# A hybrid attention block on one core: the gate and up products of the FFN on scaled fp16 halves instead of fp32r halves

## The chip, the cores and the metric

The kernel runs on one core of a Trainium2 chip, as one program. The metric is the time of one execution on the device in microseconds (us). Three runs of the kernel before gave 3368.54, 3373.79 and 3376.36 us; the median is 3373.79. The profile is of one execution more, of 3371.81 us.

## What is computed

One layer of an encoder over 2048 tokens and 16 meta tokens that are put ahead of them, 1024 wide, all in float32. The reference, cut to its structure:

```python
h = rms_norm(x, attn_norm_g)
proj = h @ w_in                        # 1024 -> 2304
out_a = grouped-query attention        # 8 query heads, 2 key/value heads, 64 wide
out_b = differential attention         # 4 heads of two 64-wide halves, values 128 wide
x = x + concat(out_a, out_b) @ w_out   # 1024 -> 1024
h = rms_norm(x, ffn_norm_g)
g = h @ w_gate                         # 1024 -> 2816
u = h @ w_up                           # 1024 -> 2816
x = x + (silu(g) * u) @ w_down         # 2816 -> 1024
return x without the meta tokens
```

## The kernel before

The kernel has four stages, one after the other: the input projection with norms and rotary embedding, the attention, the output projection (lines 1204 to 1261) and the FFN (lines 1262 to 1350). The change touches the last two.

**Products in halves.** A float32 product is made of three products of halves: each operand is kept as a rounded copy ("high") and the rest ("low", the operand minus the copy), and high x high, low x high and high x low are summed in PSUM; low x low is left out. In the attention the halves are fp16, with values scaled into its range. In the projections and the FFN they are fp32r, the four-byte type that TensorE takes in one pass. `split` (line 114) forms them: a cast on one engine (line 112 is the copy) and a subtraction on another (line 116). `transpose_split` (line 124) does so behind a transpose on TensorE (line 129).

**Output projection.** It goes through 16 tiles of 128 tokens (`for t in range(NT)`, line 1231). `load_t` (line 369) has SP load the mixed attention rows (mix_scr) and x of a tile, 512 KB each, into two pairs of buffers. `prep` (line 1215), for tile t+1 while tile t is multiplied, scales the rows on ACT (line 1216), squares half of them (line 1218), normalises that half on VectorE and POOL (lines 1220 to 1224), and transposes and splits the rows. A tile's products are 48 matmuls of 128x512 (line 1240) in two halves of 512 columns; VectorE adds x (line 1251). The first 8 tiles of y stay in SBUF, are normalised by `norm` (line 1198, with the FFN's gain g2, loaded once on line 1213) and turned into `h2h` and `h2l` (lines 1181 and 1182), the transposed halves that are the moving operand of the FFN. The last 8 tiles go to HBM (y_scr, line 1261) for the second half of the FFN.

**FFN.** Two passes (b) of 1024 tokens, each through 22 blocks (f) of 128 columns of w_gate and w_up. For a block `wload` (line 1278) has SP load three weight tiles of 512 KB (gate, up, down) and forms their halves, with the cast on ACT and the subtraction on POOL. For each half of 512 tokens (n) gate and up are 24 matmuls each of 128x512 (line 1332): 8 slices of the 1024-wide input, three terms each. The weights are the stationary operand, h2h and h2l the moving one. Tanh on ACT (line 1334) and two operations on VectorE (lines 1335 and 1336) make silu(g) * u, which is split again. The products with w_down (line 1293) of block f-1 follow, in groups of three, each ended by an addition to y on VectorE (line 1295). In numbers: 2 x 22 x 2 x 2 x 24 = 4224 matmuls on line 1332 and 2112 on line 1293.

```python
for ps, w in ((pg, wg), (pu, wu)):
    for k in range(KD):
        for ii, (a, b_) in enumerate(((w[0], hh[n]), (w[0], hl[n]), (w[1], hh[n]))):
            T.matmul(ps, a[:, k], b_[:, k], start=(k == 0 and ii == 0), stop=(k == KD - 1 and ii == 2))
th = tp4.tile([P, 512], F32, name="th4")
A.activation(th, pg, AF.Tanh, scale=0.5)
```

**What sets the order.** The attention's order is written by a planner in the file, which ends before the output projection. From there on each engine's order is fixed when the program is built, from the order of the text and a model of what is ready when; work may be put far ahead of its place in the text where a buffer is free (the loads of y_scr on line 1308 stand in block 17 of the text and are issued in block 0). On the chip each engine goes through its order strictly. SP issues all loads and stores of these stages in one order. Buffers of the weights go round in rings (line 1264): four for halves of gate and up (two blocks), four for raw loads, which begin with the buffers of the last two tiles of the output projection.

Of the kernel before, what the change touches and what calls it, by code (L numbers as in the profile page):

```python
# [11 lines left out]
F32 = mybir.dt.float32  # L12
F32R = mybir.dt.float32r
F16 = mybir.dt.float16
BF16 = mybir.dt.bfloat16
I32 = mybir.dt.int32
AF = mybir.ActivationFunctionType
ALU = mybir.AluOpType
AX = mybir.AxisListType
PSUM = bass.MemoryType.PSUM  # L20

P = 128
D = 1024
# [3 lines left out]
NT = S // P  # L27
NC = NT + 1
HD = 64
KD = D // P  # L30
UW = 384
DFF = 2816
# [53 lines left out]
def block_kernel(ctx: ExitStack, tc: tile.TileContext, x, meta, g1, w_in, gpack, lam4, subln,  # L86
# [27 lines left out]
    def split(hi, lo, src, hi_eng, lo_eng):  # L114
        copy(hi_eng, hi, src)
        lo_eng.tensor_tensor(out=lo, in0=src, in1=hi if hi.dtype == F16 else hi.bitcast(F32), op=ALU.subtract)  # L116
# [261 lines left out]
    with ExitStack() as ph:  # L378
# [774 lines left out]
        while True:  # L1153
# [11 lines left out]
            t, n, z = best  # L1165
# [10 lines left out]
    with ExitStack() as ph:  # L1176
# [1 line left out]
        TB = NT // 2  # L1178
        HT = TB // 2
        y = {t: yp.tile([P, D], F32, name=f"y{t}") for t in range(TB)}  # L1180
        hh = [yp.tile([P, KD, HT * P], F32R, name=f"h2h{i}") for i in range(2)]
        hl = [yp.tile([P, KD, HT * P], F32R, name=f"h2l{i}") for i in range(2)]
        g2_sb = yp.tile([P, D], F32, name="g2_sb")

        def normed(np_, yt, h):
# [19 lines left out]
        with ExitStack() as p3:  # L1205
# [6 lines left out]

            SP.dma_start(g2_sb, g2.partition_broadcast(P))

            def prep(t, mx):
                A.activation(mx[:, :512], mx[:, :512], AF.Copy, scale=ivs)
                sq = sqp.tile([P, 512], F32, name="sq")
                A.activation(sq, mx[:, 512:], AF.Square)
                ss = sm.tile([P, 4], F32, name="ss3")
                V.tensor_reduce(ss, sq.rearrange("p (h d) -> p h d", d=P), axis=AX.X, op=ALU.add)  # L1220
                rs = inv_rms(sm, ss, ivn, P, 4, "b")
                bv = mx[:, 512:].rearrange("p (h d) -> p h d", d=P)
                V.tensor_tensor(out=bv, in0=bv, in1=rs.unsqueeze(2).broadcast_to([P, 4, P]), op=ALU.mult)
                V.scalar_tensor_tensor(bv, bv, ivs, gb.unsqueeze(1).broadcast_to([P, 4, P]), op0=ALU.mult, op1=ALU.mult)
                mh, ml = halves(ering[t % 2])
                transpose_split(psT, mx, P, mh, ml)
                return mh, ml
# [2 lines left out]
            pend = []  # L1230
            for t in range(NT):
                mh, ml, xt = cur
                if t + 1 < NT:
                    if t + 1 not in mxt:
                        load_t(t + 1, SP)
                    nxt = mxt[t + 1]
# [25 lines left out]
        with ExitStack() as p4:  # L1262
# [4 lines left out]
            def place(ring, shape, dtype):  # L1267
                tag = rings[ring].pop(0)
                rings[ring].append(tag)
                return slot(tag, shape, dtype)  # L1270
# [6 lines left out]

            def wload(src, name):
                dn = name == "d"
                w = place("d" if dn else "w", [P, 2, 1, D] if dn else [P, 2, KD, P], F32R)  # L1280
                raw = place("r", [P, 1, D] if dn else [P, KD, P], F32)
                SP.dma_start(raw[:, 0] if dn else raw, src)
                split(w[:, 0], w[:, 1], raw, A, G)
                return w[:, 0], w[:, 1]

# [26 lines left out]
            for b in range(2):  # L1312
                for f in range(NF):
# [8 lines left out]
                    for n in range(2):  # L1322
# [8 lines left out]
                                for ii, (a, b_) in enumerate(((w[0], hh[n]), (w[0], hl[n]), (w[1], hh[n]))):  # L1331
                                    T.matmul(ps, a[:, k], b_[:, k], start=(k == 0 and ii == 0), stop=(k == KD - 1 and ii == 2))  # L1332
                        th = tp4.tile([P, 512], F32, name="th4")
                        A.activation(th, pg, AF.Tanh, scale=0.5)  # L1334
                        V.scalar_tensor_tensor(th, th, 1.0, pg, op0=ALU.add, op1=ALU.mult)
                        V.scalar_tensor_tensor(th, th, 0.5, pu, op0=ALU.mult, op1=ALU.mult)
                        split(ah[:, ns], al[:, ns], th, A, G)
                        if b == 0 and f == NF - 1:
                            for t in range(TB + n * HT, TB + (n + 1) * HT):
# [82 lines left out]
```

## Time and profile before

| what | us |
|---|---|
| median of 3 runs | 3373.79 |
| lowest and highest run | 3368.54, 3376.36 |
| profiled execution | 3371.81 |
| its span in the profile | 3369.9 |
| TensorE busy in it | 3211.7 |
| VectorE, ACT, POOL busy | 2051.8, 1488.2, 1660.6 |

The profile counts an engine as busy while an instruction of it is under way. Matmuls are pipelined: one record lasts from its start to its own end, some 395 ns for 128x512 in fp32r, while the next begins much earlier. What a matmul takes of the engine is therefore read as the distance of two starts in an unbroken run, or as the length of such a run by its count. The granted clock of TensorE is given as a share of the upper of its two levels, 2.4 GHz. A wait is put down to what came last by the profile.

### The profile page before, as it was taken

What the parts mean: (1) busy time and instruction counts of PE and PEld (TensorE: products, weight loads), DVE (VectorE), ACT (ScalarE), POOL (GpSimd) and SP (SyncE); (2) the same over time, 40 slices, a digit from 0 to 9 for tenths busy, and PEclk for the clock granted to TensorE, in tenths of its full rate; (3) what the DMA queues carried; (4) which work ended last, traced back from release to release, by engine and by line L of the source; (5) the groups of instructions that cost most, each with busy time, mean ns of one, the idle gap of its engine ahead of it and who ended that gap; (6) DMA issues with size and microseconds to landing.
All of it is one profiled execution on the core that took longest, in us unless ns stands there. A gap on an engine that the chain in (4) does not pass through costs nothing.

```text
span 3369.9 us, 57645 instructions
## 1 busy us (share of the span) xinstructions
PE 3211.7 (95%) x23041; PEld 2483.7 (74%) x23041; DVE 2051.8 (61%) x3640; ACT 1488.2 (44%) x1839; POOL 1660.6 (49%) x1596
## 2 busy tenths in 40 slices
PE   9999988989988998888799999999999999999999
PEld 7999975555555555555588888888887888888887
DVE  7555578888889888888764244444445434444445
ACT  6333338988887788788732211111112211111110
POOL 6887867776676777767510323232323232323231
PEclk9999989999999999999899999999999999999999
DMA  5222232443443334333533411111112411111111
GB/s 174 69 69 67 61 87 69 87 108 77 94 114 75 72 92 103 75 85 77 124 116 119 132 38 57 38 57 38 57 38 69 155 46 44 50 44 51 43 44 50
DMA packets 498749, 258.27 MB, mean 77 GB/s; under 512 B 330192, under 2 KB 478112, under 8 KB 497968
## 3 DMA queue, kind: packets, MB, share of 16 engines
q1 hardware_dynamic: 496768, 252.07, 28.3%
q8 instruction: 181, 2.97, 0.4%
q10 hardware_dynamic: 1712, 2.51, 0.3%
q14 instruction: 88, 0.72, 0.1%
HBM read 145.38 MB, written 39.93 MB: 55 GB/s over the span
## 4 chain that ended last, share of the span: by engine, by line
PE 77%; DVE 11%; ACT 6%; issue 4%; DMA 2%; POOL 1%; SPq 0%; DVEq 0%; ACTq 0%; POOLq 0%
PE pg L1332 29%; PE psd L1293 14%; PE pl L269 11%; PE ps L1240 5%; PE sy L482 4%; PE ob L594 3%; PE oa L570 3%; DVE e L489 3%; ACT et L555 2%; DVE mna L502 2%; PE sy L498 2%; PE sy L512 2%; DVE e L536 2%; PE sy L513 2%; PE pt L129 1%
## 5 line engine op out<-in xcount | busy, mean ns | idle before, releaser
L1295 DVE TENSOR_TENSOR y<-psd,y 128x512 f32<-128x512 f32 x704 | 484.9, 691 | 607.5 <-PE psd L1293 604.8
L1332 PE MATMUL pg<-h2h,e 128*128 128x512 f32 x2112 | 692.4, 395 | 0.0
L561 POOL TENSOR_TENSOR hl<-et,hl 128x1024 f16<-128x1024 f32 (+1 forms) x247 | 520.2, 2125 | 307.8 <-ACT hl L112 177.7
L1332 PEld LDWEIGHTS pg<-h2h,e 128*128 128x128 f32 x2112 | 396.8, 188 | 96.0
L1332 PE MATMUL pg<-h2l,e 128*128 128x512 f32 x1056 | 417.4, 395 | 0.0
L1334 ACT ACTIVATE th<-pg 128x512 f32<-128x512 f32 x88 | 52.6, 598 | 816.5 <-PE pg L1332 814.5
L116 POOL TENSOR_TENSOR e<-qa,e 128x1024 fp32r<-128x1024 f32 x44 | 106.4, 2417 | 516.2 <-issue 426.3
L489 DVE CUSTOM_DVE_ANT_0 e<-sy,zero,mn 128x1024 f32<-128x1024 f32 x256 | 325.7, 1277 | 42.7 <-PE sy L482 37.6
L555 ACT ACTIVATE et<-sy,lnpa,ndq 128x1024 f32<-128x1024 f32 (+1 forms) x288 | 321.9, 1144 | 42.2 <-PE sy L513 22.3
L549 POOL TENSOR_TENSOR p<-e,p 128x516 f16<-128x516 f32 (+2 forms) x320 | 311.1, 1004 | 50.1 <-ACT p L112 48.9
L502 DVE TENSOR_REDUCE mna<-sy 128x1 f32<-128x1024 f32 x256 | 311.5, 1218 | 16.4 <-PE sy L498 15.8
L482 PE MATMUL sy<-kt,qb 128*128 128x512 f16 (+1 forms) x1280 | 284.2, 342 | 30.2 <-DVE mn L489 9.9
L570 PEld LDWEIGHTS <-hl 128*128 128x128 f16 (+1 forms) x6528 | 241.9, 98 | 95.9 <-issue 23.9
L517 ACT ACTIVATE e<-e,bs,ndq 128x2064 f32<-128x2064 f32 x128 | 269.2, 2103 | 92.3 <-DVE bs L522 92.1
L116 POOL TENSOR_TENSOR kt<-qb,kt 128x1024 fp32r<-128x1024 f32 x22 | 53.1, 2414 | 490.4 <-issue 430.1
L570 PE MATMUL oa<-va,hl 128*128 128x65 f16 (+3 forms) x6528 | 261.9, 194 | 24.7 <-DVE hl L561 9.3
L1293 PE MATMUL psd<-e,e 128*128 128x512 f32 x1056 | 282.5, 395 | 0.7 <-DVE y L1295 0.7
L1293 PE MATMUL psd<-kt,kt 128*128 128x512 f32 x1056 | 282.6, 395 | 0.0
L112 ACT CAST hl<-et 128x1024 f16<-128x1024 f32 (+1 forms) x288 | 275.8, 991 | 7.9 <-PE oa L570 6.4
L594 PEld LDWEIGHTS <-pt 128*128 128x128 f16 (+2 forms) x3200 | 201.8, 98 | 71.4 <-issue 7.4
L1332 PEld LDWEIGHTS pg<-h2l,e 128*128 128x128 f32 x1056 | 198.4, 188 | 48.2
L594 PE MATMUL ob<-vb,pt 128*128 128x128 f16 (+2 forms) x3200 | 232.9, 220 | 0.0
(208 smaller groups left out, 5917.2 us busy)
## 6 DMA issues: line engine op xcount, KB each, us to landing
qa<-in_w_gate_dram SPq DMA_DIRECT2D x22, 512.0 KB, 3.9
qa<-in_w_down_dram SPq DMA_DIRECT2D x22, 512.0 KB, 3.6
qb<-in_w_up_dram SPq DMA_DIRECT2D x22, 512.0 KB, 3.8
qa<-in_w_up_dram SPq DMA_DIRECT2D x22, 512.0 KB, 3.8
qb<-in_w_down_dram SPq DMA_DIRECT2D x22, 512.0 KB, 3.6
qb<-in_w_gate_dram SPq DMA_DIRECT2D x22, 512.0 KB, 3.8
raw<-in_w_in_dram SPq DMA_DIRECT2D x48, 192.0 KB, 3.4
xt<-in_x_dram SPq DMA_DIRECT2D x16, 512.0 KB, 3.8
```

What stands on the lines that cost most here:

```text
L269: T.matmul(ps[:rows, c0:UW], hb[:, a, k, :rows], w_at(w, ui, k)[:, c0:], start=(k == 0 and a == 0 and w == 0), stop=(k == KD - 1 and a == 1))
L482: T.matmul(y[:, (c - c0) // 512 if g_ else j, :n], qt[:, j, a, qi * P:(qi + 1) * P], kt[:, c:c + n], start=(a == 0), stop=(a == 1))
L489: V.tensor_tensor_reduce(e[:, c0:c1], src[:, :c1 - c0], zero.broadcast_to([P, c1 - c0]), 1.0, mn[:, g_ - 1:g_] if g_ else big, ALU.add, AL ...
L502: V.tensor_reduce(g["mn"][:, h, g_:g_ + 1], y.rearrange("p b n -> p (b n)"), axis=AX.X, op=ALU.min)
L549: eng.tensor_tensor(out=p[:, at + c0:at + c1], in0=st["e"][0][:, c0:c1], in1=p[:, c0:c1], op=ALU.subtract)
L555: A.activation(of(et, k), of(y, k), AF.Exp, bias=lnpa if k else lnpa[:NM], scale=ndq[:, 0:1] if k else ndq[:NM, 0:1])
L561: eng.tensor_tensor(out=of(z[:, 1], k), in0=of(et, k), in1=of(z[:, 0], k), op=ALU.subtract)
L570: T.matmul(o[:, h, :wn], z[:rows, a, i, h * P:(h + 1) * P], vt[:rows, c, vh, :wn], start=(first and h == 0 and n == 0), stop=(last and n = ...
L594: T.matmul(o, pt[:rows, blk, :], vt[:rows, c, vh, :], start=(c == 0 and n == 0), stop=(c == NC - 1 and n == 1))
L1293: T.matmul(ps, a[:, i * P:(i + 1) * P], w[:, 0, ns], start=(ii == 0), stop=(ii == 2))
L1295: V.tensor_tensor(out=yt[:, ns], in0=ps, in1=yt[:, ns], op=ALU.add)
L1332: T.matmul(ps, a[:, k], b_[:, k], start=(k == 0 and ii == 0), stop=(k == KD - 1 and ii == 2))
```

## The change

The halves of h2 become fp16 instead of fp32r, and so do the halves of the gate and up weights; the down products stay as they are. To fit fp16's range the gain g2 is scaled to 2^9 by its largest magnitude, rounded to a power of two (eight VectorE operations behind the load of g2, five of them on one column), and the weights are multiplied by a power of two, made from the sum of squares of both matrices. That sum is formed during the output projection: `squares` loads half a 128-row slice of w_gate and of w_up (128x1408 each) into one of two buffers and squares it on ACT with an accumulated sum; it is called for four slices in the first two tiles and for one in each of the next twelve, 16 calls with 32 loads. `weights_scale`, in the last but one tile, sums over partitions by a matmul with ones and forms the scale and its inverse. Each gate and up load then has one more pass on ACT that scales it in place. Tanh and the product behind it take the inverse scale as an operand instead of a constant.

```diff
-        hh = [yp.tile([P, KD, HT * P], F32R, name=f"h2h{i}") for i in range(2)]
-        hl = [yp.tile([P, KD, HT * P], F32R, name=f"h2l{i}") for i in range(2)]
+        hh = [yp.tile([P, KD, HT * P], F16, name=f"h2h{i}") for i in range(2)]
+        hl = [yp.tile([P, KD, HT * P], F16, name=f"h2l{i}") for i in range(2)]
...
+            V.tensor_reduce(gm2[:, 0:1], g2_sb, axis=AX.X, op=ALU.max)
+            V.tensor_reduce(gm2[:, 1:2], g2_sb, axis=AX.X, op=ALU.min)
...
+            V.tensor_scalar(g2_sb, g2_sb, gm2[:, 1:2], 2.0 ** 9, op0=ALU.mult, op1=ALU.mult)
+            wqp = p3.enter_context(tc.tile_pool(name="wqp", bufs=2, reuse_waits="tile"))
+            psS = p3.enter_context(tc.tile_pool(name="psS", bufs=1, space=PSUM, reuse_waits="tile"))
+
+            def squares(t):
+
+                rs_, cs_ = slice(t // 2 * P, (t // 2 + 1) * P), slice(t % 2 * (DFF // 2), (t % 2 + 1) * (DFF // 2))
+                for i, w in enumerate((w_gate, w_up)):
+                    raw = wqp.tile([P, DFF // 2], F32, name="wq")
+                    SP.dma_start(raw, w[rs_, cs_])
+                    A.activation(raw, raw, AF.Square, accum_out=wsq[:, t, i:i + 1])
+
+            def weights_scale():
+
+                tot = np3.tile([P, 1], F32, name="tot")
+                V.tensor_reduce(tot, wsq.rearrange("p t i -> p (t i)"), axis=AX.X, op=ALU.add)
+                ps = psS.tile([P, 1], F32, name="pss")
+                T.matmul(ps, allones, tot, start=True, stop=True)
+                V.tensor_scalar(tot, ps, 1e-30, None, op0=ALU.max)
+                G.tensor_tensor(out=wsc[:, 0:1], in0=tot, in1=mhalf[:, :1], op=ALU.pow)
...
+                V.reciprocal(wsc[:, 1:2], wsc[:, 0:1])
+                V.tensor_scalar(unh[:, 0:1], wsc[:, 1:2], gm2[:, 0:1], 2.0 ** -10, op0=ALU.mult, op1=ALU.mult)
+                V.tensor_scalar(unh[:, 1:2], unh[:, 0:1], unh[:, 0:1], 2.0, op0=ALU.mult, op1=ALU.mult)
...
             for t in range(NT):
                 mh, ml, xt = cur
+                for z in (2 * t, 2 * t + 1) if t < 2 else (t + 2,):
+                    if z < NT:
+                        squares(z)
+                if t == NT - 2:
+                    weights_scale()
...
-                w = place("d" if dn else "w", [P, 2, 1, D] if dn else [P, 2, KD, P], F32R)
+                w = place("d" if dn else "w", [P, 2, 1, D] if dn else [P, 2, KD, P], F32R if dn else F16)
                 raw = place("r", [P, 1, D] if dn else [P, KD, P], F32)
                 SP.dma_start(raw[:, 0] if dn else raw, src)
+                if not dn:
+                    A.activation(raw, raw, AF.Copy, scale=wsc[:, 0:1])
                 split(w[:, 0], w[:, 1], raw, A, G)
...
-                        A.activation(th, pg, AF.Tanh, scale=0.5)
+                        A.activation(th, pg, AF.Tanh, scale=unh[:, 0:1])
                         V.scalar_tensor_tensor(th, th, 1.0, pg, op0=ALU.add, op1=ALU.mult)
-                        V.scalar_tensor_tensor(th, th, 0.5, pu, op0=ALU.mult, op1=ALU.mult)
+                        V.scalar_tensor_tensor(th, th, unh[:, 1:2], pu, op0=ALU.mult, op1=ALU.mult)
```

## Rows read from the trace of the kernel before

**Rows 1.** The page, part 1: engine, busy us, share of the span, instructions.
```profile
PE 3211.7 (95%) x23041; PEld 2483.7 (74%) x23041; DVE 2051.8 (61%) x3640; ACT 1488.2 (44%) x1839; POOL 1660.6 (49%) x1596
```
**Rows 2.** The page, part 4: the chain that ended last, shares by line.
```profile
PE pg L1332 29%; PE psd L1293 14%; PE pl L269 11%; PE ps L1240 5%; PE sy L482 4%; PE ob L594 3%; PE oa L570 3%; DVE e L489 3%; ACT et L555 2%; DVE mna L502 2%; PE sy L498 2%; PE sy L512 2%; DVE e L536 2%; PE sy L513 2%; PE pt L129 1%
```
**Rows 3.** Stretches: length, then PE, PEld, DVE, ACT, POOL busy, clock, DMA share, GB/s.
```profile
1688.70:1878.10 189.40, 189.16 (x913) 155.80 (x913) 95.34 (x153) 54.88 (x93) 26.73 (x25) 1.00 0.35 116
1878.10:3369.90 1491.80, 1485.27 (x6403) 1196.56 (x6401) 624.01 (x913) 251.22 (x337) 426.70 (x227) 1.00 0.19 57
```
**Rows 4.** Groups of line 1332 by form: busy us, mean ns of one, idle before.
```profile
L1332 PE MATMUL pg<-h2h,e 128*128 128x512 f32 x2112 | 692.4, 395 | 0.0
...
L1332 PE MATMUL pg<-h2l,e 128*128 128x512 f32 x1056 | 417.4, 395 | 0.0
...
L1332 PE MATMUL pg<-h2h,kt 128*128 128x512 f32 x704 | 228.1, 395 | 0.0
...
L1332 PE MATMUL pg<-h2l,kt 128*128 128x512 f32 x352 | 139.3, 396 | 0.0
```
**Rows 5.** The chain in order of time, in the FFN: start us, us, what.
```profile
1878.75 44.82 PE pg L1332 x192
```
**Rows 6.** Timeline of TensorE in the attention: start us, us, instruction; eight starts lie between.
```profile
527.85 0.38 PE L512 MATMUL sy<-qa,kt 128*128 128x512 f16 x1 [0.29 <-ACT et L555]
...
529.57 0.62 PE L570 MATMUL oa<-va,hl 128*128 128x65 f16 x15
```
**Rows 7.** A stretch of the attention around them, columns as in rows 3.
```profile
500.00:540.00 40.00, 32.80 (x336) 18.31 (x335) 34.38 (x59) 36.29 (x35) 26.10 (x19) 0.96 0.19 45
```
**Rows 8.** The chain in order of time, in the input projection.
```profile
120.41 4.20 PE pl L269 x24
```
**Rows 9.** Groups of ACT by form: the Squares and Exp that accumulate.
```profile
L517 ACT ACTIVATE e<-e,bs,ndq 128x2064 f32<-128x2064 f32 x128 | 269.2, 2103 | 92.3 <-DVE bs L522 92.1
...
L1200 ACT ACTIVATE h_f<-y 128x1024 f32<-128x1024 f32 x8 | 8.6, 1070 | 0.0
...
L1200 ACT ACTIVATION_READ_ACCUMULATOR h_f<-y 128x1 f32 x8 | 1.6, 197 | 0.0
```
**Rows 10.** Timeline of all engines in the output projection, one tile's preparation.
```profile
1813.48 1.04 PE L129 MATMUL pt<-ident,qa 128*128 128x128 f32 x8
...
1814.58 0.32 SPq L376 DMA_DIRECT2D qa<-mix_scr  x1
...
1818.26 0.72 ACT L1216 ACTIVATE qa<-qa,ivs 128x512 f32<-128x512 f32 x1 [3.07 <-DMA qa<-mix_scr]
...
1822.41 0.75 DVE L1224 SCALAR_TENSOR_TENSOR qa<-qa,ivs,gb 128x512 f32<-128x512 f32 x1
...
1825.21 1.03 PE L129 MATMUL pt<-ident,qa 128*128 128x128 f32 x8
```
**Rows 11.** DMA from 1672 to 1700 us, in 40 slices: GB/s.
```profile
GB/s 0 59 82 228 325 229 278 290 291 290 268 223 369 398 404 334 415 416 357 170 193 359 312 382 339 380 398 410 427 392 164 47 18 0 0 0 0 0 53 135
```
**Rows 12.** The page, part 5: two of its costliest groups.
```profile
L502 DVE TENSOR_REDUCE mna<-sy 128x1 f32<-128x1024 f32 x256 | 311.5, 1218 | 16.4 <-PE sy L498 15.8
...
L594 PE MATMUL ob<-vb,pt 128*128 128x128 f16 (+2 forms) x3200 | 232.9, 220 | 0.0
```
**Rows 13.** Groups by form from 1850 us on: a VectorE operation on one column.
```profile
L120 DVE TENSOR_SCALAR rs_f<-ss_f 128x1 f32<-128x1 f32 x8 | 1.2, 154 | 9.4 <-ACT sq_f L1189 9.0
```
**Rows 14.** Timeline of ACT at the entry to the FFN.
```profile
1874.96 1.05 ACT L112 CAST e<-qb 128x1024 fp32r<-128x1024 f32 x1 [6.19 <-DMA qb<-in_w_up_dram]
...
1896.63 1.06 ACT L112 CAST e<-qb 128x1024 fp32r<-128x1024 f32 x1 [2.63 <-DMA qb<-in_w_gate_dram]
```
**Rows 15.** Timeline of TensorE where fp16 products are followed by fp32r ones.
```profile
1680.73 3.07 PE L594 MATMUL ob<-vb,pt 128*128 128x128 f16 x50
...
1683.73 0.73 PE L1240 MATMUL ps<-e,e 128*128 128x512 f32 x2
```
**Rows 16.** DMA issues from 1640 to 1900 us: KB each, median us to landing.
```profile
qa<-mix_scr SPq DMA_DIRECT2D x15, 512.0 KB, 3.6
```

More of the change, by code (lines that the diff above doesn't have):

```diff
@@ L1180, in block_kernel @@
         y = {t: yp.tile([P, D], F32, name=f"y{t}") for t in range(TB)}
-        hh = [yp.tile([P, KD, HT * P], F32R, name=f"h2h{i}") for i in range(2)]
-        hl = [yp.tile([P, KD, HT * P], F32R, name=f"h2l{i}") for i in range(2)]
+        hh = [yp.tile([P, KD, HT * P], F16, name=f"h2h{i}") for i in range(2)]
+        hl = [yp.tile([P, KD, HT * P], F16, name=f"h2l{i}") for i in range(2)]
+        gm2 = yp.tile([P, 2], F32, name="gm2")
+        wsc = yp.tile([P, 2], F32, name="wsc")
+        unh = yp.tile([P, 2], F32, name="unh")
+        allones = yp.tile([P, P], F32, name="allones")
+        V.memset(allones, 1.0)
+        wsq = yp.tile([P, NT, 2], F32, name="wsq")
         g2_sb = yp.tile([P, D], F32, name="g2_sb")
@@ L1213, in block_kernel @@
             SP.dma_start(g2_sb, g2.partition_broadcast(P))
+            V.tensor_reduce(gm2[:, 0:1], g2_sb, axis=AX.X, op=ALU.max)
+            V.tensor_reduce(gm2[:, 1:2], g2_sb, axis=AX.X, op=ALU.min)
+            V.tensor_scalar(gm2[:, 1:2], gm2[:, 1:2], -1.0, None, op0=ALU.mult)
+            V.tensor_tensor(out=gm2[:, 0:1], in0=gm2[:, 0:1], in1=gm2[:, 1:2], op=ALU.max)
+            V.tensor_scalar(gm2[:, 0:1], gm2[:, 0:1], 1e-15, None, op0=ALU.max)
+            V.tensor_scalar(gm2[:, 0:1].bitcast(I32), gm2[:, 0:1].bitcast(I32), 0x7F800000, None, op0=ALU.bitwise_and)
+            V.reciprocal(gm2[:, 1:2], gm2[:, 0:1])
+            V.tensor_scalar(g2_sb, g2_sb, gm2[:, 1:2], 2.0 ** 9, op0=ALU.mult, op1=ALU.mult)
[14 more added lines that the diff above has]
+                G.tensor_tensor(out=wsc[:, 0:1], in0=tot, in1=mhalf[:, :1], op=ALU.pow)
+                V.tensor_scalar(wsc[:, 0:1].bitcast(I32), wsc[:, 0:1].bitcast(I32), 0x7F800000, None, op0=ALU.bitwise_and)
+                V.tensor_scalar(wsc[:, 0:1], wsc[:, 0:1], 2.0 ** 15, None, op0=ALU.mult)
+                V.reciprocal(wsc[:, 1:2], wsc[:, 0:1])
+                V.tensor_scalar(unh[:, 0:1], wsc[:, 1:2], gm2[:, 0:1], 2.0 ** -10, op0=ALU.mult, op1=ALU.mult)
+                V.tensor_scalar(unh[:, 1:2], unh[:, 0:1], unh[:, 0:1], 2.0, op0=ALU.mult, op1=ALU.mult)
             def prep(t, mx):
```

## The prediction, made before the changed kernel ran

> **What bounds the kernel now.** I read the page's engine totals first, then its chain of waits, then the busy times by stage, and only then single instructions. The totals put TensorE at 95% of the span, far ahead of VectorE's 61% [rows 1]. The chain says the same by line: its largest share, 29%, is line 1332, the gate and up products, and the next four are TensorE's too [rows 2]. The stages say where that is the limit. From 1878.1 us to the end (the FFN) TensorE is busy 1485.27 of 1491.80 us at a granted clock of 1.00, the upper of its two levels, 2.4 GHz, while VectorE has 624, POOL 427 and ACT 251 us; in the output projection before it (1688.7 to 1878.1) it is busy all but 0.24 of 189.4 us [rows 3]. In the FFN nothing that shortens another engine can help, and what shortens a matmul helps in full. In the output projection other engines have room, but a small one if they are late: there TensorE waits for nothing now.
>
> The number of gate and up products is read from the groups of line 1332: 2112 + 1056 + 704 + 352 = 4224, each 128x512 [rows 4]. The 395 ns that a group gives is the latency of one; they are pipelined, so the price of one is the distance between two starts. The chain has a piece of 192 of them in a row, 44.82 us: 0.2334 us each [rows 5].
>
> **What the type costs.** The attention stage has fp16 matmuls of the same shape, each with a stationary tile of its own, as here. Eight in a row start between 527.85 and 529.57: 1.72 / 8 = 0.2150 us [rows 6]. In the 40 us around them VectorE is busy 34.4, ACT 36.3 and POOL 26.1 us, so traffic of other engines does not lengthen these, and the FFN, with less of it, has the slower ones [rows 3, 7]. That the 0.0184 us belongs to fp32r itself is seen at another width: 24 fp32r matmuls of 384 columns take 4.20 us, 0.1750 each [rows 8]. Per column this is 0.456 ns, against 0.456 ns at 512 in fp32r and 0.420 ns in fp16. An excess that grows with the columns lies in the streaming of the moving operand, and the change makes that operand (hh, hl) fp16 as well as the weights.
>
> So the FFN should lose 4224 x (0.2334 - 0.2150) = 77.7 us. The 2112 down products keep fp32r and their price. The two starts that give the fp16 distance are read to 0.01 us, which is 0.0012 us in eight, or 5 us in the sum.
>
> By the Trainium skill (TensorE: Matmul & The Clock Gate, section Weight-path perf modes) the array processes one element per cell and cycle regardless of element width, and its section Back-to-back issue gap gives 512 / 2.4 + 2.5, about 216 ns, for any type. The fp16 rows agree with that; the fp32r rows (233 ns) don't. By the page nothing would be gained, and the sum would be the added costs alone.
>
> **What is added, part by part.**
>
> *Sum of squares.* 32 loads of 128x1408 fp32 (0.72 MB, 23.1 MB in all) on SP's queue and 32 Squares on ACT. A Square with its accumulator is 1.07 + 0.20 us at 1024 elements and 2.10 at 2064 in an ACTIVATE [rows 9]; between them 1408 elements take 1.07 + 384 x 0.99 ns + 0.20 = 1.65 us, so 3.3 us of ACT a tile and 53 us in all. ACT is busy 54.9 of 189.4 us there [rows 3], so it has room. What counts is the loop that prepares the next tile [rows 10]: SP issues the load of the mixed rows at 1814.58, when the transposes of the tile before have freed the buffer; ACT scales them at 1818.26; VectorE's last step is done at 1822.41 + 0.75 = 1823.16; TensorE, in order, transposes at 1825.21. The spare is 2.05 us of a tile's 11.73 (1825.21 - 1813.48). Everything that the new work puts in front of the scaling beyond 2.05 us is idle time of TensorE. SP also gets a new wait: a load of weights waits until the Square two loads earlier has freed one of two buffers, and behind it stand the mixed rows, x and the stores of y_scr. On ACT a Square waits for its load, and behind it stand the scaling and the casts of the transposes.
>
> The bounds: nothing, if the loads run in the free time (the stage moves 116 GB/s [rows 3], and slices of the hand-over before it reach 427 [rows 11]) and the Squares fall into ACT's idle time; or two Squares in front of each scaling, 3.3 - 2.05 = 1.25 us for 15 tiles, 19 us. I take 8: the loads are free to run ahead of their tiles as far as two buffers allow, but a fixed order on ACT will be wrong in some tiles.
>
> *Gain of g2.* Two reductions of 128x1024 at 1.22 us [rows 12], one scaling of the same size, taken as 1.22 too, and five operations on one column at 0.15 [rows 13], 4.4 us of VectorE, once, when the first tiles are late anyway. 0 to 4.4; I take 2.
>
> *The scale itself* (weights_scale): a reduction, a one-column matmul, a power on POOL and five small steps in a chain, in the last but one tile, some 25 us before the FFN. It is on the path only where TensorE reaches its matmul early: 0 to 1, I take 0.5.
>
> *One ACTIVATE more for each gate and up load*: 88 passes of 128x1024, at 1.05 us if they cost what the cast does [rows 14], or 0.72 + 512 x 0.99 ns = 1.23 by the scaling of line 1216 [rows 10]: 92 to 108 us of ACT. ACT has 1240 us free in the FFN [rows 3], and the weights' buffers hold two steps of f, so in the steady state this costs nothing; its cover is TensorE's 32 us a step. The lower halves that POOL forms and the casts get a narrower output: no bound but ACT's and POOL's idle time, 0. At the entry there is no cover. The first up weights are cast at 1874.96 [rows 14]; with the scaling (1.1), the cast (1.05) and POOL's 2.4 they are ready at 1879.5, and TensorE wants them 24 matmuls after 1878.1, at 1883.3: no cost. The gate weights of f=1 are cast at 1896.63 after a late load [rows 14], so whole at 1901.2, while TensorE will have done its first 96 at 1878.1 + 96 x 0.215 = 1898.7: up to 2.5 us once, I take 1.5.
>
> Tanh and the two products after it change scalars only: 0. Half-size h2h and h2l make room for the new buffers: 0.
>
> **The sum** is against the profiled execution, 3371.81 us, of which 3369.9 are the span; the median of the runs shown is 2.0 higher and the lowest 3.3 lower, so it stands for them. 3371.8 - 77.7 + 8 + 2 + 0.5 + 1.5 = 3306.1, say 3306.
>
> **Rivals.**
> (a) *The distance is not the type's.* Should it be set by the mix of this stage, fp16 changes nothing and the costs remain: 3371.8 + 12 = 3384. For it: only the FFN's stage shows 128x512 back to back for long, and every one in it is slow. Against it: the same shape in fp16 and the other width in fp32r [rows 6, 8]. Chance 0.06. This is also what the Trainium skill's rule, named above, would make of it.
> (b) *Switching types.* The down products stand between the others in groups of three (one tile of PSUM), so TensorE changes from fp16 to fp32r up to 2112 / 3 = 704 times, 470 if groups often come in pairs. One such step can be seen: 50 fp16 products of 128 columns from 1680.73, 3.07 us to the end of the last, whose own latency is 0.22 [rows 12, 15]. Their distance is 2.85 / 49 = 0.058, so the next could start at 1683.64; the first fp32r one does at 1683.73. 470 x 0.09 = 42: 3348. Against it: under a 512-column matmul there is more time to load the next weights. Chance 0.08.
> (c) *The queue.* Two weight loads ahead of the mixed rows in each tile, 2 x 0.72 MB at 427 GB/s [rows 11] = 3.4 us, and both Squares: 6.7 - 2.05 = 4.65 us, 15 times: 70 us, so 3371.8 - 77.7 + 70 + 4 = 3368. Chance 0.06.
> (d) *ACT blocked, slower than before.* A Square stands at the head of ACT's order before its data are there. The load of 0.5 MB lands after 3.6 us [rows 16]; one of 0.72 MB after some 4.5 by my estimate. If each tile's scaling waits for this, for both Squares and for the queue, it is 4.5 + 3.3 + 3.4 - 2.05 = 9.2 us, 15 times: 138, and 3371.8 - 77.7 + 138 + 4 = 3436. It decides where the scaling starts more than 77.7 / 15 + 2.05 = 7.2 us later after the transposes than now. Against it: the Squares have no consumer until the last tiles, and can run whenever data are there. Chance 0.04.
>
> **The numbers.** The forecast has 0.76. Its range goes from the costs at nothing with the 5 us of the reading, 3289, to half of (c)'s 70 us with the smaller costs at their bounds, 3371.8 - 77.7 + 35 + 8 = 3337; beyond lie (a), (b), (d) and part of (c), 2 in 10. 0.2%, 7 us, is about what a measurement tells from no change. Faster: 0.76, (b) and half of (c), 0.87. Same: half of (c) and a third of (a), 0.05. Slower: the rest of (a) and (d), 0.08.
>
> **What would show it.** Right: pieces of line 1332 in the chain at 0.215 us a matmul, down products still at 0.233, the FFN some 76 us shorter, the output projection between 189 and 210 us. Wrong: line 1332 still at 0.233 (a); a gap at each change of line (b); TensorE idle before the transposes, put down to the load of the mixed rows (c) or to ACT waiting for a weight load (d).

## The result, and the profile after

The changed kernel takes 3310.43 us (median of 4 runs, 3309.67 to 3313.47) against 3372.76 in the runs of the kernel before beside them: a ratio of 0.9817, 95% interval 0.9800 to 0.9834. The profiled execution took 3310.24 us, its span 3308.4. The median is 4.4 us above the forecast of 3306 and inside its range.

Line numbers have moved: the gate and up products are line 1379 (1332 before), the down products 1340 (1293), the output projection's products 1285 (1240). The page, parts 1 and 4 (columns as in [rows 1, 2]):

```profile
PE 3145.7 (95%) x23043; PEld 2069.5 (63%) x23043; DVE 2056.2 (62%) x3656; ACT 1639.2 (50%) x1991; POOL 1639.3 (50%) x1597
...
PE pg L1379 27%; PE psd L1340 14%; PE pl L269 10%; PE sy L482 4%; PE ob L594 4%; PE oa L570 3%; DVE e L489 3%; ACT et L555 2%; DVE mna L502 2%; PE ps L1285 2%; PE sy L498 2%; PE sy L512 2%; PE sy L513 2%; DVE e L536 2%; DMA wq<-in_w_up_dram 1%
```

TensorE still sets the end, by the same lines, but a new item stands in the chain: a load of the sum of squares. The two stages, measured from the first product of the output projection to the first gate product and from there to the end (columns as in [rows 3]):

```profile
1673.10:1884.50 211.40, 205.75 (x1004) 166.13 (x1004) 104.80 (x176) 105.84 (x166) 26.97 (x26) 0.99 0.68 235
1884.50:3308.40 1423.90, 1417.40 (x6401) 783.94 (x6400) 627.59 (x913) 357.58 (x424) 403.03 (x227) 1.00 0.19 60
```

The output projection of the kernel before; its FFN took 1491.3 us (1878.6 to 3369.9, nearly the second stretch of [rows 3]):

```profile
1673.20:1878.60 205.40, 204.84 (x1003) 167.48 (x1004) 101.40 (x160) 61.81 (x101) 27.31 (x26) 0.98 0.40 129
```

So the FFN lost 67.4 us and the output projection gained 6.0; what lies ahead of them is the same program and ends 0.1 us earlier. 67.4 - 6.0 + 0.1 = 61.5 is the difference of the two spans. All later runs are compared by these two lengths. The attention ahead of them ended anywhere from 1671.6 to 1683.5 us in kernels whose text is the same up to there, so a whole span of one execution is a worse measure than its stages. Numbers with two decimals of a stage, and mean distances over many starts, are worked out from the starts of the instructions in the trace.

The chain in order of time, in the FFN, and a piece of TensorE's timeline where the lines change (start us, us, what):

```profile
1957.57 2.39 PE pg L1379 x11
1959.96 1.40 PE psd L1340 x6
```

```profile
2105.12 0.38 PE L1379 MATMUL pg<-h2h,e 128*128 128x512 f16 x1
2105.15 1.74 PE L1340 MATMUL psd<-kt,kt 128*128 128x512 f32 x6
2106.73 0.39 PE L1379 MATMUL pg<-h2h,e 128*128 128x512 f16 x1
2106.96 0.38 PE L1379 MATMUL pg<-h2l,e 128*128 128x512 f16 x1
2107.17 0.59 PE L1379 MATMUL pg<-h2h,e 128*128 128x512 f16 x2
```

Eleven gate and up products now take 2.39 us, 0.217 each; the down products stay at 1.40 / 6 = 0.233. The timeline shows why it is 0.217 and not 0.215: behind the fp32r group the first two fp16 starts are 2106.96 - 2106.73 = 0.23 apart, the next 0.21. Over all starts of the FFN in the records, an fp16 product that follows an fp16 one is 0.2159 us from the next, an fp32r one 0.2331 before the change. In the record the first fp32r product starts 0.03 us behind the last fp16 one, so a single start there is no measure; a whole run, from the fp16 start ahead of it to the second one behind it, is. A run of three fp32r products takes 1143.4 ns that way where 2 x 215.9 + 3 x 233.3 = 1131.7 are expected; a run of six takes 9.5 ns too long. There are 437 runs; the 420 of three, six or nine with fp16 products on both sides are 10.9 ns too long on average: some 4.7 us in all.

TensorE's waits, the three largest in the output projection that are new or larger, and the one in the FFN that is new (of the rest, 1.1 us for ACT's e stands in the trace of before too, 0.5 us for VectorE's kt does not; before, the wait for ACT's cast of line 112 was 0.5 us):

```profile
PE ps L1285 <- DVE e L116: 1.9, 1, 1.9
PE pt L129 <- DVE e L116: 1.3, 3, 0.5
PE ps L1285 <- ACT e L112: 1.3, 1, 1.3
...
PE pg L1379 <- POOL e L116: 1.6, 1, 1.6
```

The loads issued from 1672 to 1889 us (KB each, us to landing; [rows 16] has 3.6 us for the mixed rows):

```profile
wq<-in_w_gate_dram SPq DMA_DIRECT2D x16, 704.0 KB, 4.9
wq<-in_w_up_dram SPq DMA_DIRECT2D x16, 704.0 KB, 5.4
qb<-in_x_dram SPq DMA_DIRECT2D x16, 512.0 KB, 5.7
qa<-mix_scr SPq DMA_DIRECT2D x15, 512.0 KB, 5.1
```

Most of it is lost early: up to 1736 us TensorE is busy 58.20 of 62.90 us, where it had 62.24 of 62.80 before, and afterwards all but 1 us. The first line is the kernel before:

```profile
1673.20:1736.00 62.80, 62.24 (x318) 49.87 (x319) 38.15 (x59) 24.54 (x39) 10.10 (x9) 0.95 0.53 170
1673.10:1736.00 62.90, 58.20 (x299) 45.99 (x300) 37.52 (x62) 37.52 (x57) 8.31 (x8) 0.96 0.88 304
1736.00:1884.50 148.50, 147.55 (x707) 120.15 (x705) 67.28 (x115) 68.31 (x109) 18.66 (x18) 1.00 0.59 206
```

Late rows alone cost little: of the loads issued from 1740 to 1790 us the mixed rows land after 6.4 us, and TensorE is idle for less than 1 us in all that time.

The longest of the waits, 1.9 us, can be followed (all engines, around 1700 us):

```profile
1699.32 1.21 DVE L1222 TENSOR_REDUCE gm<-g_sb 128x1 f32<-128x1024 f32 x1
1700.45 1.21 DVE L1223 TENSOR_REDUCE gm<-g_sb 128x1 f32<-128x1024 f32 x1
1701.57 1.28 DVE L116 TENSOR_TENSOR e<-pt,e 128x512 fp32r<-128x512 f32 x2
1702.31 0.74 PE L1285 MATMUL ps<-e,e 128*128 128x512 f32 x2 [1.92 <-DVE e L116]
```

The two reductions of g2 (2.25 us up to 1701.57) stand in VectorE's order ahead of the split of the next tile, for which TensorE waits.

### The profile page after: what moved, and what is told of

It reads as the page before. It is cut to its first block, busy times and chain, and to the rows that moved or that the text cites. A ratio compares the mean times of both kernels' runs of the same rounds, so it can differ in the third digit from the quotient of the medians.

```text
span 3308.4 us, 57942 instructions
## 1 busy us (share of the span) xinstructions
PE 3145.7 (95%) x23043; PEld 2069.5 (63%) x23043; DVE 2056.2 (62%) x3656; ACT 1639.2 (50%) x1991; POOL 1639.3 (50%) x1597
## 3 DMA queue, kind: packets, MB, share of 16 engines
q10 hardware_dynamic: 1712, 2.51, 0.3%
## 4 chain that ended last, share of the span: by engine, by line
PE 72%; DVE 11%; ACT 6%; issue 5%; DMA 4%; POOL 1%; SPq 0%; DVEq 0%; ACTq 0%; POOLq 0%
PE pg L1379 27%; PE psd L1340 14%; PE pl L269 10%; PE sy L482 4%; PE ob L594 4%; PE oa L570 3%; DVE e L489 3%; ACT et L555 2%; DVE mna L502 2%; PE ps L1285 2%; PE sy L498 2%; PE sy L512 2%; PE sy L513 2%; DVE e L536 2%; DMA wq<-in_w_up_dram 1%
## 5 line engine op out<-in xcount | busy, mean ns | idle before, releaser
L1379 PE MATMUL pg<-h2h,e 128*128 128x512 f16 x2112 | 660.0, 380 | 1.6 <-POOL e L116 1.6
L1379 PEld LDWEIGHTS <-e 128*128 128x128 f16 x3168 | 283.2, 98 | 390.3 <-issue 84.9
L1379 PE MATMUL pg<-h2l,e 128*128 128x512 f16 x1056 | 400.7, 380 | 0.0
L116 POOL TENSOR_TENSOR e<-qa,e 128x1024 f16<-128x1024 f32 (+1 forms) x44 | 100.0, 2273 | 498.8 <-issue 381.8
L1381 ACT ACTIVATE th<-pg,unh 128x512 f32<-128x512 f32 x88 | 60.5, 688 | 532.3 <-PE pg L1379 525.4
L1340 PE MATMUL psd<-kt,kt 128*128 128x512 f32 x1056 | 323.0, 434 | 0.0
L1340 PE MATMUL psd<-e,e 128*128 128x512 f32 x1056 | 320.5, 432 | 0.7 <-DVE y L1342 0.7
L1340 PEld LDWEIGHTS psd<-e,e 128*128 128x128 f32 x1056 | 198.8, 189 | 59.0 <-DVE y L1342 1.2
L1340 PEld LDWEIGHTS psd<-kt,kt 128*128 128x128 f32 x1056 | 199.0, 189 | 58.5
```

What stands on the lines that cost most here:

```text
L1340: T.matmul(ps, a[:, i * P:(i + 1) * P], w[:, 0, ns], start=(ii == 0), stop=(ii == 2))
```

## The experiments

Each line: the median, the ratio to the kernel before on the same chip, the two stages of the profiled run; of the output projection also the time in which TensorE was idle and the time in which its clock was granted at the lower of its two levels, 1.2 GHz, both in us.

| run | median us | ratio (95%) | output projection us | TensorE idle in it | lower clock in it | FFN us |
|---|---|---|---|---|---|---|
| kernel before | | | 205.4 | 0.5 | 6.6 | 1491.3 |
| changed kernel | 3310.43 | 0.9817 (0.9800-0.9834) | 211.4 | 5.6 | 4.8 | 1423.9 |
| e1_fp32r | 3368.94 | 0.9981 (0.9972-0.9991) | 206.1 | 2.1 | 3.2 | 1484.3 |
| e2_noscan | 3305.48 | 0.9800 (0.9785-0.9814) | 205.1 | 0.9 | 4.7 | 1424.9 |
| e3_loads | 3311.00 | 0.9814 (0.9800-0.9829) | 209.5 | 5.0 | 3.3 | 1424.0 |
| e4_squares | 3308.76 | 0.9806 (0.9792-0.9821) | 206.6 | 0.9 | 6.6 | 1422.8 |
| e5_down16 | 3274.66 | 0.9697 (0.9677-0.9718) | 212.5 | 5.8 | 6.7 | 1385.9 |
| e6_shift | 3366.93 | 0.9975 (0.9964-0.9987) | 206.1 | 1.2 | 6.6 | 1484.9 |
| e7_actqueue | 3320.05 | 0.9836 (0.9816-0.9855) | 219.7 | 13.3 | 3.3 | 1424.2 |
| e8_nopass | 3314.38 | 0.9820 (0.9792-0.9847) | 213.3 | 7.7 | 4.5 | 1425.7 |
| e9_spread | 3312.85 | 0.9819 (0.9803-0.9836) | 211.6 | 3.9 | 11.5 | 1424.1 |
| e10_down16_spread | 3272.51 | 0.9697 (0.9682-0.9711) | 212.7 | 5.0 | 11.5 | 1384.9 |
| e11_half | 3311.76 | 0.9813 (0.9797-0.9829) | 209.4 | 4.6 | 4.2 | 1424.1 |
| e12_shift32 | 3370.09 | 0.9984 (0.9973-0.9995) | 205.1 | 0.9 | 4.7 | 1485.8 |

Between the variants of the output projection the intervals overlap; there the stage lengths, of one execution each, are the evidence. How fine they are is seen in e5, which goes through this stage in the changed kernel's order (ACT's last steps apart) and takes 1.1 us longer, and in e8, whose squares are those of the changed kernel and whose stage is 1.9 us longer, by another order of the steps: differences under 2 us in this column say little. Part of such a difference is the clock, which is at its lower level when the stage begins, for a time that differs from execution to execution (TensorE has just waited 5.6 us for VectorE there). At that level the products of this stage stand 0.43 us apart instead of 0.23 (starts in e9, below), so 2 us more of it make the stage some 0.9 us longer, by an estimate from these two distances. The idle time leaves that out.

**Types back (e1) and no sum of squares (e2).**

```diff
-        hh = [yp.tile([P, KD, HT * P], F16, ...
+        hh = [yp.tile([P, KD, HT * P], F32R, ...
...
-                for z in (2 * t, 2 * t + 1) if t < 2 else (t + 2,): ...
...
-                G.tensor_tensor(out=wsc[:, 0:1], in0=tot, in1=mhalf[:, :1], op=ALU.pow)
+                V.memset(wsc[:, 0:1], 256.0)
```

(e2 has the lower two edits alone; in e1 hl and the weights' halves are fp32r as well. The scale is a constant in e3, e4, e8 and e11 too.)

> The halves of h2 and of the gate and up weights are fp32r again; the rest of the change stays, except the sum of squares, for whose buffers there is no room beside them: its 32 loads and 32 Squares are left out and the weights' scale is the constant 256. If the distance of two matmuls belongs to the type, the gate and up products stand 0.233 us apart again, the FFN takes 1491 to 1494 us and the whole 3372 to 3375 us. If the gain came from something else that the change brought (the scaled values, the order built for it, other buffers), the time stays near 3304 us and the distance near 0.216.

> The changed kernel (fp16) without the sum of squares: no weight loads and no Squares in the output projection, the scale is the constant 256. If the 6.0 us that the output projection has become longer are the price of the sum of squares, this stage takes 205.4 us again (211.4 with it), the FFN stays at 1424, and the whole is 3304 us. If they are the price of the scaling of g2 or of another order of the instructions, the stage stays at 211 and the whole at 3310. Against the run with fp32r of the same call the difference is the type alone: 4224 x 0.0184 = 77.7 us by the distances, some 70 if each change between the types costs 0.015 us about 470 times.

With the types back the FFN is at 1484.3 us and the distance at fp32r's: the gain is the type's, and rival (a) falls. But it is 7.0 us below the kernel before, which neither theory expected. The chain in order of time shows a first stretch of 0.2315 us a product where [rows 5] have 0.2334, and eleven products with weights in kt at 2.51 / 11 = 0.228:

```profile
1882.42 44.44 PE pg L1360 x192
...
1988.07 2.51 PE pg L1360 x11
```

So between e1 and e2, equal but for the type (and for the places of y and the halves, which are half as wide in fp16), the FFN differs by 59.4 us, not 70; what moved e1 is found below (e6, e12). In e2 the output projection is at 205.1 us, as before the change: the 6.0 us are the sum of squares and what it does to the order around it. The scaling of g2 is still in e2 and costs nothing there that can be seen, so its 1.9 us in the changed kernel is a matter of where the order puts it.

**Loads alone (e3), Squares alone (e4).**

```diff
-                    A.activation(raw, raw, AF.Square, accum_out=wsq[:, t, i:i + 1])
+                    A.activation(raw[:, :8], raw[:, :8], AF.Square, accum_out=wsq[:, t, i:i + 1])
```

> The 32 weight loads stay, each Square takes 8 of the 1408 columns only, the scale is the constant 256 (the sum of squares is left out). If the loads cost the time (the queue of SP, the shared bandwidth, late mixed rows), the output projection stays near 211 us and the whole near 3310. If the Squares on ACT do, the stage is 205.4 to 207 us and the whole 3304 to 3306.

> The 32 Squares of 1408 columns stay, but on a tile that is set once, with no weight loads; the scale is the constant 256 (the sum of squares is left out). If ACT's time costs the 6 us, the output projection stays near 211 us and the whole near 3310; if the loads cost it, the stage is near 205.4 us and the whole near 3304.

(e4 has no loads: its Squares read one tile that is set once.) Against e2 the loads alone cost 209.53 - 205.05 = 4.5 us, the Squares alone 206.56 - 205.05 = 1.5: together 6.0, and both at once, in the changed kernel, 6.3. The 1.5 is no wait: TensorE is idle for 0.9 us in e4 as in e2, and the clock was at its lower level for 6.6 us instead of 4.7, some 0.9 of the 1.5. With the loads alone it is idle for 5.0 us. So the loads make TensorE wait, and the Squares by themselves do not. In e3 TensorE waits for the split of the transposes, and the mixed rows land late; in e4 neither shows:

```profile
PE pt L129 <- DVE e L116: 3.3, 4, 1.3
```

```profile
qb<-in_x_dram SPq DMA_DIRECT2D x16, 512.0 KB, 5.4
qa<-mix_scr SPq DMA_DIRECT2D x15, 512.0 KB, 5.2
```

```profile
qa<-mix_scr SPq DMA_DIRECT2D x15, 512.0 KB, 3.7
```

**Down products in fp16 too (e5).**

```diff
-                w = place("d" if dn else "w", [P, 2, 1, D] if dn else [P, 2, KD, P], F32R if dn else F16)
+                w = place("d" if dn else "w", [P, 2, 1, D] if dn else [P, 2, KD, P], F16)
...
-                if not dn:
-                    A.activation(raw, raw, AF.Copy, scale=wsc[:, 0:1])
+                A.activation(raw, raw, AF.Copy, scale=2.0 ** 10 if dn else wsc[:, 0:1])
...
-                        V.tensor_tensor(out=yt[:, ns], in0=ps, in1=yt[:, ns], op=ALU.add)
+                        V.scalar_tensor_tensor(yt[:, ns], ps, 2.0 ** -16, yt[:, ns], op0=ALU.mult, op1=ALU.add)
```

> The changed kernel with the down products in fp16 too: act and w_down have fp16 halves, act is scaled by 2^6 in the product that takes the inverse scale, w_down by 2^10 in one more ACT pass for each of its 44 loads, and the addition to y multiplies by 2^-16. The records of the kernel before and after the change give a mean distance of 0.2333 us for fp32r and 0.2159 for fp16, and an excess of 0.0107 us for each of 441 runs of down products between fp16 ones. If the distance belongs to the type and the excess to the change between types, 2112 x 0.0174 = 36.7 and 441 x 0.0107 = 4.7 us go: 3310.4 - 41.4 = 3269 us, and no start after a change of line is late any more. If the excess belongs to the change of line (other PSUM tiles, another moving operand), it stays: 3274. If the addition with a multiplication is slower on VectorE and TensorE waits for PSUM, or the down weights come late by the added pass, it is more than that.

The halves of act become fp16 and one scale changes as well. (The expectation counts 441 runs; the starts have 437, which leaves the 4.7 us.) The first theory holds. In the chain nine down products take 1.94 us (0.216), and in the timeline the first start after them is as regular as the rest (2107.69 + 2 x 0.216 = 2108.12):

```profile
1928.71 1.94 PE psd L1339 x9
1930.65 3.67 PE pg L1378 x17
```

```profile
2106.39 1.46 PE L1339 MATMUL psd<-kt,kt 128*128 128x512 f16 x6
2107.69 0.59 PE L1378 MATMUL pg<-h2h,e 128*128 128x512 f16 x2
2108.12 0.38 PE L1378 MATMUL pg<-h2l,e 128*128 128x512 f16 x1
```

So the 4.7 us belong to the change of type, not to the change of line. From first to last start of the FFN 39.9 us went where 41.4 were expected; 1.3 of the rest is a new wait, of the transposes for the second half of the tokens:

```profile
PE pt L129 <- DVE h2l L116: 1.3, 2, 0.7
```

By the medians e5 takes 35.8 us less than the changed kernel, by the ratios of the table some 40, as the two ran beside other runs of the kernel before; by the spans of the profiled runs it is 37.4. 3269 was too low by 5.7 us: 1.5 lie in the FFN, 1.1 in the output projection, which is longer here (1.9 us more at the lower clock), and 1.9 behind the last product, where the last stores end later.

**The place of the operands (e6, e12).** Both are the kernel before with an unused tile, of 184 and of 8 columns:

```diff
         hl = [yp.tile([P, KD, HT * P], F32R, name=f"h2l{i}") for i in range(2)]
+        shift = yp.tile([P, 184], F32, name="shift")
+        V.memset(shift[:, :1], 0.0)
```

> The kernel before with nothing but an unused tile of 736 bytes per partition behind h2l, so that y, h2h and h2l lie 736 bytes lower, at the places they have in the run with fp32r halves and without the sum of squares (e1_fp32r). That run's FFN took 1484.3 us with fp32r throughout, 7.0 less than the kernel before, and its products with the weights in kt stood 0.228 us apart instead of 0.2326. If the distance in fp32r depends on where the operands lie, the FFN takes 1484.3 us here too and the whole some 3367 us. If the scaled values or the other order of the instructions made it, the FFN stays at 1491.3 and the whole at 3373 us.

> The kernel before with an unused tile of 32 bytes per partition behind h2l instead of 736 (e6_shift). Before, h2h and h2l begin 32 bytes behind a multiple of 64; with 736 bytes and with 32 they begin at a multiple of 64. If that alignment sets the distance in fp32r, the FFN takes 1484 to 1485 us here as in e6_shift and the whole some 3367. If the distance to other tiles counts (or a larger stride), it lies elsewhere, at 1491 or at a third value.

Both FFNs are 5.5 to 6.5 us shorter than before, with nothing computed otherwise. The first 192 products in the chain of each:

```profile
1884.47 44.45 PE pg L1334 x192
```

```profile
1877.05 44.34 PE pg L1334 x192
```

That is 0.2315 and 0.2309 us a product. TensorE goes through the same 6400 products in the same order in both and in the kernel before, and e6's mean distances agree with e1's to 0.1 ns in each of the eight largest groups of products. So e1's 7.0 us are the place of y, h2h and h2l, the only tiles that moved, and neither the scaled values nor the order. That a start at a multiple of 64 bytes is what counts fits both totals, but not the details: the products with weights in kt stand 0.228 to 0.230 apart in e6 and 0.233 in e12, those with weights in e the other way round (0.233 and 0.231). Nor is it only what a product reads: the down products with both operands in e, which did not move, came from 233.3 ns before to 231.2 in e6 and 232.3 in e12. VectorE adds to y beside them, and y moved; whether that is the reason, and which places are slow, stays open. In fp16 (changed kernel, e5) no group of more than ten starts is off 0.2158 by more than 0.0002, except behind a change of type; but no run moved the fp16 operands.

**Loads from ACT's queue (e7).**

```diff
-                    SP.dma_start(raw, w[rs_, cs_])
+                    A.dma_start(raw, w[rs_, cs_])
```

> The changed kernel with the 32 loads for the sum of squares issued by ACT instead of SP; nothing else differs in the text. SP waited 73.1 us for Squares to free a buffer, with the mixed rows and x behind. If that blocked queue makes the mixed rows late, the output projection goes back from 211.4 to some 207 us (205.1 without squares, and 1.5 for ACT's Squares) and the whole to 3306. If the shared transfers do (the mixed rows land after 5.1 us instead of 3.6), it stays at 210 to 211 and the whole at 3310. If ACT's own order is hurt by the issues, it is longer than 211.

8.3 us worse: the third case, and TensorE is idle for 13.3 us instead of 5.6. ACT's casts of the transposes come late now,

```profile
PE pt L129 <- DVE e L116: 4.5, 5, 1.5
PE ps L1285 <- ACT e L112: 4.5, 5, 2.8
```

and x and the mixed rows still take 4.9 us from issue to landing, with SP's queue free of the weights: the transfers lengthen each other, whichever queue issues the weights. A landing time counts from the issue, so it does not tell what SP's blocked order costs by issuing the rows late; ACT's lateness covers that here, and it stays open.

**Without the scaling pass (e8).**

```diff
-                if not dn:
-                    A.activation(raw, raw, AF.Copy, scale=wsc[:, 0:1])
```

> The changed kernel without the ACT pass that scales each gate and up load (the scale is the constant 1, so the weights' halves are formed unscaled). If the pass is hidden in the steady state and costs only the wait at the gate weights of f=1 (1.6 us), the FFN goes from 1423.9 to 1422.3 us and the whole to 3309. If it also slows the steady state, by taking ACT's time or by traffic in SBUF, the distance in fp16 falls below 0.2159 and the FFN gets shorter by more; if the wait at f=1 comes from the late load and not from the pass, nothing changes.

The steady state does not get faster (1419.3 us from the first start to the last, as in the changed kernel; that its FFN is 1.8 us longer lies behind the last product), so the 88 passes (1.15 us each) are hidden. But the wait at f=1 stays, so the pass was not its cause either:

```profile
PE pg L1370 <- POOL e L116: 1.8, 1, 1.8
```

By the expectation an unchanged wait would mean the late load. The trace says otherwise: in e8 ACT does not cast the gate weights when they have landed (1904.2), but behind the cast of act's first half, for which it waits 3.59 us for VectorE:

```profile
1906.71 0.62 ACT L112 CAST e<-th 128x512 fp32r<-128x512 f32 x1 [3.59 <-DVE th L1374]
1907.24 1.04 ACT L112 CAST e<-qb 128x1024 f16<-128x1024 f32 x1
```

It is POOL's lower half of the gate weights that TensorE waits for. In the changed kernel's timeline the cast is done at 1904.23 + 1.04 = 1905.27, POOL is free at 1906.90, behind its half of act, and then the subtraction takes 3.12 us where the next takes 2.12. VectorE's gain for the second half of the tokens lies beside both and takes 2.29 where the one before took 1.28:

```profile
1900.96 1.28 DVE L1198 SCALAR_TENSOR_TENSOR kt<-kt,rs_f,g_sb 128x1024 f32<-128x1024 f32 x1 [0.73 <-POOL rs_f L121]
...
1904.23 1.04 ACT L112 CAST e<-qb 128x1024 f16<-128x1024 f32 x1
...
1905.68 1.28 POOL L116 TENSOR_TENSOR e<-th,e 128x512 fp32r<-128x512 f32 x1
1905.74 2.29 DVE L1198 SCALAR_TENSOR_TENSOR kt<-kt,rs_f,g_sb 128x1024 f32<-128x1024 f32 x1 [2.78 <-POOL rs_f L121]
...
1906.90 3.12 POOL L116 TENSOR_TENSOR e<-qb,e 128x1024 f16<-128x1024 f32 x1
1909.98 2.12 POOL L116 TENSOR_TENSOR e<-qa,e 128x1024 f16<-128x1024 f32 x1
```

That is read from the trace; no run takes the gain or act's half out of the way.

**Spread or fewer loads (e9, e10, e11).** In e9 a Square takes a scale of 1.0 that VectorE makes from the tile before; e10 is that with e5's edits; e11 leaves out every second slice.

```diff
-                for z in (2 * t, 2 * t + 1) if t < 2 else (t + 2,):
+                if t:
+                    one = prog[:, t - 1:t]
+                for z in ((2 * t - 2, 2 * t - 1) if t < 4 else (t + 2,)) if t else ():
...
-                    A.activation(raw, raw, AF.Square, accum_out=wsq[:, t, i:i + 1])
+                    A.activation(raw, raw, AF.Square, scale=one, accum_out=wsq[:, t, i:i + 1])
```

> The changed kernel with the sum of squares tied to the tiles: no slice in the first tile, two in each of the next three, one in each of the ten after them, and each Square takes a scale of 1.0 that VectorE makes from the tile before, so that it can't run ahead; the loads run ahead by two buffers at most. In the changed kernel all 32 Squares were done after some 128 of the stage's 211 us, and DMA moved 250 to 400 GB/s in that time. If the crowd makes the mixed rows and x late, the output projection falls from 211.4 to some 207 us (205.1 without any, 206.6 with Squares but no loads) and the whole to 3306. If each load costs the same wherever it stands, or a Square that has to wait holds up ACT's casts, it stays at 211 or goes above.

> The down products in fp16 as in e5_down16 (3274.7 us) with the sum of squares tied to the tiles. If spreading the loads gives back 4 to 5 us of the output projection's 212.4, 3270 us; if it gives nothing, 3275; if Squares that wait hold up ACT, above 3278.

> The changed kernel with every second slice of the sum of squares left out: 16 loads and 16 Squares, the scale is the constant 256. If each load and Square costs its share, the output projection takes 205.1 + 6.3 / 2 = 208.2 us and the whole 3307. If the cost comes from the crowd of the first tiles (four slices there, now two), most of it goes: 206 us and 3305.

Spread out, the loads leave the stage as long as it was (211.6 us), and e10's is no different from e5's. By that my theory of the crowd falls; by the waits it falls in part. The mixed rows land sooner than with the crowd, in 4.4 us, and TensorE is idle for 3.9 us instead of 5.6 (5.0 for 5.8 in e10), with other waits in the old ones' place:

```profile
PE pt L129 <- DVE h2l L116: 1.8, 1, 1.8
...
PE ps L1290 <- ACT e L112: 1.0, 1, 1.0
```

But it is busy for 207.7 us instead of 205.8. Behind the wait of 1.8 us, which ended at 1716.85, the granted clock was at its lower level until 1724.0, which it was not in the changed kernel, and the products there start 0.43 us apart:

```profile
1671.60:1883.16 211.56, 207.67 (x1005) 168.26 (x1005) 106.36 (x192) 109.81 (x166) 25.33 (x26) 0.97 0.68 234
1717.00:1724.20 7.20, 6.18 (x21) 4.75 (x21) 4.22 (x7) 5.64 (x10) 0.56 (x1) 0.53 0.92 330
```

```profile
1720.17 0.63 PE L1290 MATMUL ps<-kt,e 128*128 128x512 f32 x1
1720.60 0.63 PE L1290 MATMUL ps<-e,e 128*128 128x512 f32 x1
```

Half the loads and Squares (e11) cost 209.4 - 205.1 = 4.3 us, between the 3.2 of half the price and all of it, which one execution does not tell apart; e11 keeps the 1.9 us behind g2's reductions, and e9 does not have it:

```profile
PE ps L1278 <- DVE e L116: 1.9, 1, 1.9
```

So the 6 us are no single wait. Shown is that the loads cause the larger part, some 4.5, and that spreading them takes away 0.8 to 1.7 us of TensorE's idle time, which the clock took back. How the rest divides between late landings, SP's order and the places that the order then gives to VectorE's and ACT's steps stays open.

## Why the prediction was right, point by point

**The distance: right in kind, 5 us too large.** 4224 x (0.2331 - 0.2159) = 72.7 us in place of 77.7. The fp16 price was read from eight starts (0.2150), and the forecast gave that reading 5 us; the fp32r one (0.2334) came from a stretch that was a little slower than the mean. That it is the moving operand's type, as the prediction argued, is not shown: the weights change type with it (a weight load takes 98 ns in fp16 and 188 in fp32r), and no run changes one of the two alone. The fp32r price is not one number either: with the operands elsewhere it is 0.231 (e1, e6, e12), and the same change would have gained some 7 to 8 us less from there (e1 to e2: 59.4 in the FFN, for 67.4). The Trainium skill (TensorE: Matmul & The Clock Gate, section Back-to-back issue gap) gives N / 2.4 + 2.5 ns, about 216 for 512 columns, and makes no difference between types; every fp16 row here agrees (215.8), no fp32r row does. (For a sustained stream the section has some 131 ns, which no row here shows.)

**Switching types: missing in the sum.** The forecast had it only as rival (b), at 0.09 us a time and 42 us. It is there, at some 0.011 us, an eighth of that, and only on the way back to fp16: 4.7 us. (b)'s 0.09 was read from one start of an fp32r product behind fp16 ones, which is no measure: in the FFN the record puts such a start 0.03 us behind its forerunner. e5 shows that the price is the type's. That the rest is hidden under a 512-column product, as the text argued against (b), fits but is not shown.

**Sum of squares, g2 and the scale: 6.0 for 8 + 2 + 0.5.** The guess of 8 for the loop was near in size: 6.3 by e2, g2's reductions in their bad place among it. Its reason was not: it stood for Squares that ACT's fixed order puts in front of a scaling, while the loads were taken as free to run ahead. With the Squares alone (e4) TensorE waits no longer than without them, 0.9 us; with the loads alone (e3) it waits 5.0. So that this term came near is luck. In a good place (e2) g2 and the scale cost nothing that can be seen. A Square takes 1.38 + 0.18 us where 1.65 was taken. SP waited 73.1 us for Squares to free a buffer; what that cost the rows behind it was not separated. (c) and (d) needed each tile to wait; the three waits of TensorE make 4.5 us in all, mostly in the first tiles. `weights_scale` had its matmul at 1813.55, 71 us ahead of the FFN.

**Entry: 1.6 for 1.5, for another reason.** The step that failed is the one that put it on the late load and the scaling: without the pass it is 1.8 us. By the trace POOL's subtraction beside VectorE's gain, behind the halves of act, makes it, so the near number is luck here too.

**ACT's pass: nothing, as forecast.** It is 88 x 1.15 = 101 us of ACT, in the bounds of 92 to 108.

The sum of what was found, against the profiled execution: 3371.8 - 72.7 + 4.7 + 6.0 + 1.6 - 0.1, and 1.5 us less between the last product and the end (4.6 for 6.1), is 3309.8; it took 3310.2. Against the forecast, the distance and the switching made it 9.7 us too low, and the sum of squares with g2 and the scale, and the end, 6.0 too high. That it came within 4 to 5 us owes something to these cancelling; the range of 48 us did not need it.

## What to carry to other kernels

Where TensorE is the bound, the distance of two starts in an unbroken run is the price that counts, and it should be read from hundreds of starts: eight starts, read to 0.01 us, made 3.8 us of the forecast's largest error, the 5 us of the distance. Changing one of two product groups that alternate leaves a price at each change of type; changing both (e5) took 3.0% off the kernel before, where the change alone took 1.8%. A stage whose engines look half idle can still have no room: 23 MB of loads with slack in every total cost some 4.5 us, and neither another queue nor an even spread gave it back. And a stage that begins at the lower clock should be compared by TensorE's idle time beside its length: between two executions the clock alone moved it by some 1 us, by the estimate above.

## What the runs showed of the hardware that was not expected

In fp32r the distance of 128x512 products depends on where tiles lie: 0.2334 us in the first stretch of the kernel before, 0.2315 and 0.2309 with y and the moving operand 736 or 32 bytes lower, 0.228 for some pairs, and 0.2312 for 0.2333 (e6) even where neither operand moved. In fp16 it was 0.2158 or 0.2159 in every group, in places that no run changed. The first fp16 product behind an fp32r group starts 0.2264 us before the next instead of 0.2159. And a subtraction on POOL took 3.12 us instead of 2.12, and VectorE's gain 2.29 instead of 1.28, where the gain ran beside that subtraction and POOL's step ahead of it. It is not always both that lose: in e8 a gain that began at 1902.67, 0.07 us behind a POOL subtraction, took 3.35 us, and the subtraction its usual 2.34.
